# A transformer block in float32 halves: the first 52 feed-forward weight tiles are split ahead of time and kept in DRAM, and the first V step follows 36 U steps instead of 44

## The chip, the cores and the metric

The kernel runs on one core of a Trainium2 chip. The metric is the device time of one execution in microseconds (us). Before the change the median of three runs is 1940.61 us (1940.46 to 1943.16).

A core has four engines that compute here. TensorE (PE in the rows; PEld is its weight load) multiplies matrices, VectorE (DVE) and GpSimd (POOL) work on elements, and ScalarE (ACT) applies functions and copies. SyncE (SP) issues most of the DMAs. Each engine works through its own queue in order and waits on semaphores for the others.

## The reference, cut to what matters

One block of a diffusion transformer: 512 latent tokens and 256 context tokens of 1024 features. A token mixer (an mLSTM in both directions, a window attention, two branch gates) gives the new residual x1. The feed-forward part that the change is about picks experts by product keys, per token and head, and sums their outputs:

```python
def block(xb):                                   # 128 tokens
    q = (xb @ w_query).reshape(128, 8, 2, 128)
    s = jnp.einsum('mhpd,hpnd->mhpn', q, sub_keys)
    s1, i1 = lax.top_k(s[:, :, 0], 16)
    s2, i2 = lax.top_k(s[:, :, 1], 16)
    ...                                          # the 16 best of the 256 sums of pairs
    top, pos = lax.top_k(cand, 16)
    idx = jnp.take_along_axis(cidx, pos, axis=-1)
    g = jax.nn.softmax(top, axis=-1)
    act = jax.nn.gelu(jnp.einsum('mhkd,md->mhk', expert_u[idx], xb))
    return jnp.einsum('mhk,mhkd->md', g * act, expert_v[idx])
```

There are 128 x 128 = 16384 experts, each a row of u and a row of v of 1024 features.

## The kernel before, in words

Every large product is made in float32 precision from two halves. A weight tile of 128 x 1024 is loaded raw (512 KB), its high half is a rounded copy made by ScalarE, its low half is the difference, made by VectorE or GpSimd. Three matmuls (high by high, low by high, high by low; `mm3`, lines 161 to 164) then stand for one. Raw tiles lie in the tag `wraw` with 4 buffers (`WR`), high halves in `whi` with 3 and low halves in `wlo` with 3. The mixer and the feed-forward part share these buffers.

The mixer (lines 96 to 671) has no order written by hand: a planner takes, of the instructions that can run, the one that comes first in the code. A load of weights can run as soon as a raw buffer is free, so loads come early and wait for buffers. The mixer's weight tiles are, in this order, those of the input projection (`project`, `gate_proj`; line 230 and line 581), 8 of the merge (line 624) and 8 of w_out (line 659). Then x1 is normed and split into `h2hi`, `h2lo`.

From line 740 on each engine works in the order of emission. TensorE's order is `stream` (lines 675 to 680): 16 Q steps (query columns of one half head), then `N1 + 2` = 46 U steps (u of 128 experts by 384 tokens, 24 matmuls), then V 44, U 46, V 45, U 47 and so on in pairs (V: v of 128 experts, 18 matmuls), and at last the V steps that have no U beside them: 126, 127 and 0 to 43. The activations of the first `N1` U tiles (`gelu`, line 1025) are stored to DRAM in groups of four and read again for their V.

A step's tile is loaded four steps ahead (`load`, `LA`), and split two steps ahead by `high` (ScalarE, line 701) and `low` (line 707). `low` works on GpSimd for the first 60 steps and on VectorE afterwards.

VectorE's work beside the steps is emitted by generators, along three estimated clocks (`clk`): `background` finds the 16 best of each list (`top16`, lines 771 to 778; 24 calls), `choose` (line 810) turns places into expert numbers and weights for each of the four blocks of 128 tokens, and `weights` (line 865) builds one-hot rows for three blocks, which TensorE multiplies in 48 groups of 16 small matmuls (line 921). The result, a weight for each dense token and each expert, goes through DRAM (`Gd`). `choose` lets GpSimd make one product (line 838) for three of the four blocks. No V step can begin before all weights are there. The fourth block's tokens are not dense: for them the 128 + 128 chosen rows of u and v are gathered one by one (`gather`, `rows`), spread over the V steps at an estimated 3.1 us each, and VectorE works on each row (lines 999 and 1007).

Of the kernel before, what the change touches and what calls it, by code (L numbers as in the profile page):

```python
# [3 lines left out]

# [24 lines left out]
SB = 1  # L29
N1 = 44  # L30
# [3 lines left out]
LA, GB = 4, 6  # L34


def body(ctx, tc, A, out):
# [43 lines left out]
    class Pair:  # L81
        """[128, 8, n] as two tiles of four chunks"""
# [92 lines left out]
    a1 = cst.tile([128, 16], F32, name="a1")     # gain, gain of the context  # L175
# [47 lines left out]
    aqd = dr.tile([128, NB, 512], F32, name="aqd")      # waits for the attention  # L223
    nc.sync.dma_start(aqd, aqt)
# [1 line left out]
    def wtiles(src, col, n, eng=None):  # L226
        """src [1024, ncols] -> four tiles [128, 2, n] raw, split in two."""
# [8 lines left out]
    def project(col, n, feat, tok, eng=None):  # L236
        """feat: list of (feature-tile offset) computed as [feat, T] for the latent tokens;
        tok: list of blocks computed as [tok, n]"""
# [17 lines left out]

    kT = ga([128, NH, T], F32, "kT")
    pf, _ = project(cK, 512, range(4), [], G)
    for h in range(4):
        S.activation(kT[:, h], pf[h], AF.Copy, scale=KSCALE)  # L260
# [9 lines left out]
    # gates, attention k and v (token layout)  # L270
# [15 lines left out]
    # log sigmoid of the forget gates, li and lf zero-padded by direction  # L286
    zz = wk.tile([128, 6, 2, 2, 8], F32, name="zz", bufs=1)  # blk, dir, kind, (dir h)
# [46 lines left out]
    # back to columns; (dir, quantity, head) on the free axis  # L334
# [9 lines left out]
    # natural order: by block, for the backward direction un-reversed  # L344
    ct = cst.tile([128, 6, 2, 4, 4], F32, name="ct")     # blk, dir, quantity, head
# [18 lines left out]
    # mlstm k, v  # L364
# [29 lines left out]
    for h in range(4):  # L394
# [38 lines left out]
        adas(16 + 3 * h, 19 + 3 * h)  # L433
    den = wk.tile([128, 2, 4, 4], F32, name="den", bufs=1)
# [31 lines left out]
    # rotation tables with the gains in: (q, k), (cos, sin), block, 64  # L466
# [8 lines left out]
    # queries and keys as exact halves stacked on the contraction axis:  # L475
    # kv head 0 has [hi; lo], kv head 1 has [lo; hi]
# [45 lines left out]
    for n in range(4):  # L522
        # keys in the order context, previous block, own block, next block
# [6 lines left out]
        mx = wk.tile([128, 4, 8], F32, name="mx", tag="mx")   # max, -max, den, sink term  # L530
# [42 lines left out]
        adas(28 + 5 * n, 33 + 5 * n)  # L573

# [3 lines left out]
    def gate_proj(col, dst):  # L578
        """sigmoid of 128 columns of the input projection, feature layout"""
# [10 lines left out]
    # o gate, then m (feature layout)  # L590
    sigo = gate_tile("sigo")
    for h in range(4):
        gate_proj(cO + h * 128, sigo[:, h])
    g_m = load_const("g_mlstm", [128, 4])
# [9 lines left out]
    # the branch gates wait in DRAM  # L604
    sgd = dr.tile([8, 128, 2, T], F32, name="sgd")
    for n in range(8):
        for br in range(2):
            st = gen.tile([128, T], F32, name="sgs", tag="SGS", bufs=2)
            gate_proj(cG + br * 1024 + n * 128, st)
            nc.sync.dma_start(sgd[n, :, br], st)  # L610

    V.tensor_tensor(out=mod[:, 16:48], in0=mod[:, 16:48], in1=b_ada[:, 16:48], op=ALU.add)

# [4 lines left out]
    for n in range(8):  # L618
# [23 lines left out]
        split(zh[n // 4][:, n % 4], zl[n // 4][:, n % 4], z0)  # L642
    g1 = mod[:, 16:24]
    x1T = Pair(F32, T, "x1T")
    x1d = dr.tile([128, 4, D], F32, name="x1d")     # token layout, for the end
# [40 lines left out]
    raws, his, los = {}, {}, {}  # L686

    def load(j):
        if j >= NS:
            return  # L690
        kind, i = stream[j]
        t = raws[j] = wp.tile([128, 1024], F32, name="wraw", tag="wraw", bufs=WR)
# [5 lines left out]
    def high(j):  # L698
        if j < NS:
# [3 lines left out]
    def low(j):  # L703
        if j < NS:
            los[j] = wp.tile([128, 1024], F32R, name="wlo", tag="wlo", bufs=3)
            pool = j < 16 + N1
            (G if pool else V).tensor_tensor(out=los[j], in0=raws.pop(j), in1=his[j].bitcast(F32), op=ALU.subtract)  # L707
            if pool:
                clk["P"] = max(clk["P"], clk["T"]) + 2.2
            else:  # L710
                clk["D"] = max(clk["D"], clk["T"]) + 1.1

    for j in range(LA):
        load(j)
    for j in range(3):
        high(j)
        low(j)
# [6 lines left out]
    TS = SB * 128                       # tokens whose experts are gathered  # L724
    TD = T - TS                         # tokens that meet every expert
# [41 lines left out]
    def top16(srcs, val, idx):  # L767
        """the 16 largest, in order, of each row of srcs [128, 4, n]"""
# [41 lines left out]
    def choose(b):  # L810
        """the 16 experts of each head for block b -> [128 tokens, (i1, i2, weight), 128 picks]"""
# [19 lines left out]
        # one-hot of the list position, laid out [head, list position, pick]  # L831
        ohs = []
        for c in range(2):
# [3 lines left out]
            eng = V if b == ORDER[0] else G  # L837
            eng.tensor_tensor(out=oh, in0=oh, in1=idv[:, :, c, :, None].to_broadcast([128, 8, 16, 16]), op=ALU.mult)
            if eng is G:
                clk["P"] = max(clk["P"], clk["D"] + 1.2) + 4.3  # L840
            ohs.append((oh, clk["P"] if eng is G else 0.0))
            yield 1.15 if eng is G else 2.3
# [6 lines left out]
        for c, (oh, ready) in enumerate(ohs):  # L849
            yield ("until", ready + 0.3)  # L850
# [11 lines left out]
    peq = deque()                        # (estimated time, PE work)  # L862
    actq = deque()

    def weights(b):
        pick = picks[b]
        w = pa_([128, 4, 128], F16, "pT16", bufs=2)
        we = pa_([128, 128], BF16, "pTe", bufs=2)
        st = {}

        def tr():
# [3 lines left out]
            return 0.4  # L875

        def tr2():
            p = st["p"]
            S.activation(w[:, 0:2], p[:, 0:2], AF.Copy)
            gs = st["gs"] = pa_([128, 128], F32, "gs")  # L880
# [440 lines left out]
```

## Time and profile before

| | before |
|---|---|
| median of three runs | 1940.61 us |
| span of the profiled execution (no other time of it is given) | 1938.4 us |
| mean granted TensorE clock | 0.966 |
| busy: TensorE / VectorE / ScalarE / GpSimd | 1789.8 / 1491.4 / 718.2 / 689.3 us |
| moved by DMA | 427 MB, 220 GB/s in the mean |
| GpSimd, low halves of line 707 | 60 instructions, 193.4 us |

Busy time of an engine is the time in which an instruction of it runs. TensorE's matmuls overlap and their ends are modelled, so the distance from one start to the next tells more than a duration. The clock is a share of 2.4 GHz. The stages of the span: the mixer up to about 594 us, the Q steps to about 690 us, U steps and one-hot products to 1040 us, pairs of V and U to 1722 us, lone V steps to 1926 us, and the last sums and stores.

### The profile page before, as it was taken

How to read it: one execution, taken by the hardware profiler on the slowest of the kernel's cores; microseconds unless marked ns; L12 is line 12 of the kernel's file. 1: busy time of each engine (PE TensorE's matmuls, PEld its weight loads, DVE VectorE, ACT ScalarE, POOL GpSimd, SP SyncE). 2: the span in 40 equal slices, each digit the busy share in tenths (PEclk: the TensorE clock that was granted, in tenths of full speed). 3: DMA queues.
4: the chain of work that ended last, by engine and by line, in shares of the span. 5: the costliest groups of instructions: out<-in, count | busy, mean ns of one | idle time of the engine just before them, and what ended most of it. 6: DMA issues, size and time to landing. Idle time of an engine off the chain costs nothing.

```text
span 1938.4 us, 24739 instructions
## 1 busy us (share of the span) xinstructions
PE 1789.8 (92%) x9039; PEld 1536.8 (79%) x9039; DVE 1491.4 (77%) x2710; ACT 718.2 (37%) x1087; POOL 689.3 (36%) x477
## 2 busy tenths in 40 slices
PE   3798998998989986889899999999999999999997
PEld 2586876555878876889799999999999999987775
DVE  7968688445647999959685777778778788878887
ACT  4242355444334333334343333333333333333332
POOL 2440254120213546546634334333333333333431
PEclk9898998999999997899999999999999999999999
DMA  8276212222533233266579888888888889889884
GB/s 348 84 248 221 86 50 83 59 66 71 169 120 129 77 103 109 93 195 202 179 220 338 319 308 318 300 315 305 315 308 310 316 302 319 302 323 349 340 346 167
DMA packets 197467, 426.97 MB, mean 220 GB/s; under 512 B 13536, under 2 KB 105312, under 8 KB 195936
## 3 DMA queue, kind: packets, MB, share of 16 engines
q1 hardware_dynamic: 109360, 257.32, 37.5%
q0 software_dynamic: 36864, 134.23, 19.3%
q10 hardware_dynamic: 51120, 33.82, 5.7%
q8 instruction: 71, 1.16, 0.2%
q14 instruction: 52, 0.43, 0.1%
HBM read 382.07 MB, written 43.25 MB: 219 GB/s over the span
## 4 chain that ended last, share of the span: by engine, by line
PE 63%; DVE 25%; issue 4%; DMA 3%; ACT 3%; POOL 2%; SPq 0%; ACTq 0%; DVEq 0%; POOLq 0%
PE pu L163 8%; PE pu L164 8%; PE pu L162 8%; PE pa L163 7%; PE pa L164 7%; PE pa L162 7%; PE pg L921 4%; PE ps L162 3%; PE ps L164 3%; PE ps L163 3%; POOL wlo L707 2%; DVE wada L119 2%; PE a L570 2%; DVE ids L774 2%; DVE tokh L1007 2%
## 5 line engine op out<-in xcount | busy, mean ns | idle before, releaser
L163 PE MATMUL pu<-h2hi,wlo 128*128 128x384 f32 (+1 forms) x1152 | 399.8, 347 | 17.0 <-POOL wlo L707 17.0
L162 PE MATMUL pu<-h2hi,whi 128*128 128x384 f32 (+1 forms) x1152 | 405.9, 352 | 6.9 <-ACT St L1032 4.2
L164 PE MATMUL pu<-h2lo,whi 128*128 128x384 f32 (+1 forms) x1152 | 399.8, 347 | 0.0
L707 DVE TENSOR_TENSOR wlo<-wraw,whi 128x1024 fp32r<-128x1024 f32 x212 | 259.5, 1224 | 135.5 <-ACT whi L701 135.0
L163 PE MATMUL pa<-whi,wl 128*128 128x512 f32 x768 | 303.4, 395 | 5.0 <-DVE wl L1048 4.1
L162 PE MATMUL pa<-whi,wh 128*128 128x512 f32 x768 | 300.7, 392 | 5.9 <-ACT wh L1044 5.8
L164 PE MATMUL pa<-wlo,wh 128*128 128x512 f32 x768 | 301.3, 392 | 0.0
L701 ACT ACTIVATE whi<-wraw 128x1024 fp32r<-128x1024 f32 x272 | 285.6, 1050 | 36.3 <-issue 23.7
L707 POOL TENSOR_TENSOR wlo<-wraw,whi 128x1024 fp32r<-128x1024 f32 x60 | 193.4, 3232 | 216.7 <-ACT whi L701 216.5
L975 POOL DMA_INDIRECT gath<-in_v,idx x128 | 155.3, 1213 | 278.5 <-DVE tokh L1007 261.6
L975 POOL DMA_INDIRECT gath<-in_u,idx x128 | 152.1, 1188 | 271.5 <-DVE gw L999 256.3
L163 PEld LDWEIGHTS pu<-h2hi,wlo 128*128 128x128 f32 x1152 | 222.0, 193 | 26.0 <-POOL wlo L707 18.2
L162 PEld LDWEIGHTS pu<-h2hi,whi 128*128 128x128 f32 x1152 | 222.4, 193 | 15.8 <-ACT St L1032 4.5
L164 PEld LDWEIGHTS pu<-h2lo,whi 128*128 128x128 f32 x1152 | 221.1, 192 | 5.5 <-DVE h2lo L50 0.4
L50 POOL TENSOR_TENSOR wlo<-wraw,whi 128x1024 fp32r<-128x1024 f32 (+1 forms) x36 | 88.7, 2465 | 265.2 <-ACT whi L49 256.3
L163 PEld LDWEIGHTS pa<-whi,wl 128*128 128x128 f32 x768 | 144.4, 188 | 40.7 <-DVE wl L1048 12.6
L162 PEld LDWEIGHTS pa<-whi,wh 128*128 128x128 f32 x768 | 144.7, 188 | 38.4 <-ACT wh L1044 10.1
L164 PEld LDWEIGHTS pa<-wlo,wh 128*128 128x128 f32 x768 | 144.6, 188 | 29.6
L1007 DVE SCALAR_TENSOR_TENSOR tokh<-gath,gw,tokh 128x1024 f32<-128x1024 f32 x127 | 162.4, 1279 | 0.0
L999 DVE CUSTOM_DVE_ANT_0 gath<-gath,tokh 128x1024 f32<-128x1024 f32 x128 | 156.1, 1219 | 2.1 <-DMA gath<-in_u,idx 2.1
L1044 ACT ACTIVATE wh<-act 128x384 fp32r<-128x384 f32 x84 | 44.2, 526 | 262.2 <-DVE act L1040 262.2
L162 PE MATMUL ps<-hhi,whi 128*128 128x512 f32 x224 | 98.0, 437 | 21.6 <-ACT hhi L49 21.6
(337 smaller groups left out, 2929.3 us busy)
## 6 DMA issues: line engine op xcount, KB each, us to landing
wraw<-in_uT SPq DMA_DIRECT2D x128, 512.0 KB, 4.9
wraw<-in_v SPq DMA_DIRECT2D x128, 512.0 KB, 6.2
Gd<-stg ACTq DMA_DIRECT2D x24, 1024.0 KB, 7.4
Gt<-Gd SPq DMA_DIRECT2D x32, 768.0 KB, 6.6
wraw<-in_w_in SPq DMA_DIRECT2D x40, 512.0 KB, 4.1
wada<-in_w_adaT SPq DMA_DIRECT2D x32, 512.0 KB, 4.4
Sd<-St ACTq DMA_DIRECT2D x11, 768.0 KB, 5.1
St<-Sd SPq DMA_DIRECT2D x11, 768.0 KB, 5.4
```

The costliest lines, as they stand in the source:

```text
L50: (eng or V).tensor_tensor(out=lo, in0=src, in1=hi.bitcast(F32), op=ALU.subtract)
L119: V.tensor_tensor_reduce(out=junk, in0=w, in1=silp[:, i], scale=1.0, scalar=0.0, op0=ALU.mult, op1=ALU.add, accum_out=col)
L162: PE.matmul(p, sh, mh, start=first, stop=False)
L163: PE.matmul(p, sl, mh, start=False, stop=False)
L164: PE.matmul(p, sh, ml, start=False, stop=last)
L701: S.activation(his[j], raws[j], AF.Copy)
L707: (G if pool else V).tensor_tensor(out=los[j], in0=raws.pop(j), in1=his[j].bitcast(F32), op=ALU.subtract)
L921: PE.matmul(p[:, ti], oa[:, ti // 4, :, ti % 4], ob[c][:, ti // 4, :, ti % 4], start=(c == 0), stop=(c == 1))
L975: G.indirect_dma_start(out=t, out_offset=None, in_=sparse["src"][s // 128], in_offset=bass.IndirectOffsetOnAxis(ap=sparse["idx"][:, s // 1 ...
L999: V.tensor_tensor_reduce(out=t, in0=t, in1=tokh[:, 0], scale=1.0, scalar=0.0, op0=ALU.mult, op1=ALU.add, accum_out=gw[:, 0, s:s + 1])
L1007: V.scalar_tensor_tensor(out=tokh[:, 1], in0=t, scalar=gw[:, 0, s - 128:s - 127], in1=tokh[:, 1], op0=ALU.mult, op1=ALU.add)
L1044: S.activation(wh, acts[i], AF.Copy)
```

## The change

Three things change.

1. `ahead(n)` makes the halves of the next n of the first `JP` = 52 steps' tiles (16 Q, 36 U): load, high half by ScalarE, low half by VectorE into the raw tile itself, and two stores to the DRAM tensor `halves`. It is called at places all through the mixer, and each of its instructions gets a place 2000 later (`LATER`) in the planner's order than where it stands. In the feed-forward part the first 52 steps load both halves from DRAM straight into `whi` and `wlo`, two steps ahead, without `high` and `low`. The later steps are as before, with `low` on VectorE alone.
2. `N1` goes from 44 to 36: 38 U steps come before the first V, 90 pairs follow, then 38 lone V.
3. VectorE makes all products of line 838, the transposes of the picks (`turn`) are emitted right after each choice, and two estimates change: a U step's eighth from 0.49 to 0.515, a group of one-hot matmuls from 1.0 to 1.9.

Comments were taken out too. The diff, cut to its core:

```diff
-N1 = 44
+N1 = 36
+JP, LATER = 16 + N1, 2000
...
+    halves = dr.tile([JP, 128, 2, 1024], F32, name="halves")
+    presplit = iter(range(JP))
+
+    def ahead(n):
+        for j in list(islice(presplit, n)):
+            with tc.high_priority(offset=-LATER):
+                raw = wp.tile([128, 1024], F32, name="sraw", tag="wraw", bufs=WR)
+                src = A["w_q"][j] if j < 16 else A["uT"][j - 16].rearrange("p k n -> p (k n)")
+                nc.sync.dma_start(raw, src)
+                hi = wp.tile([128, 1024], F32R, name="shi", tag="whi", bufs=3)
+                S.activation(hi, raw, AF.Copy)
+                V.tensor_tensor(out=raw.bitcast(F32R), in0=raw, in1=hi.bitcast(F32), op=ALU.subtract)
+                nc.sync.dma_start(halves[j, :, 0], hi.bitcast(F32))
+                nc.sync.dma_start(halves[j, :, 1], raw)
...
     pf, _ = project(cK, 512, range(4), [], G)
+    ahead(2)
...
         V.tensor_tensor(out=gk[:, b], in0=px[b][:, 256:272], in1=bg, op=ALU.add)
+    ahead(4)
...
         adas(16 + 3 * h, 19 + 3 * h)
+        ahead(4)
...
         adas(28 + 5 * n, 33 + 5 * n)
+        ahead(4)
...
         gate_proj(cO + h * 128, sigo[:, h])
+        ahead(1)
...
             nc.sync.dma_start(sgd[n, :, br], st)
+            ahead(1)
...
         split(zh[n // 4][:, n % 4], zl[n // 4][:, n % 4], z0)
+        ahead(1)
...
         kind, i = stream[j]
+        if j < JP:
+            his[j] = wp.tile([128, 1024], F32R, name="whi", tag="whi", bufs=3)
+            los[j] = wp.tile([128, 1024], F32R, name="wlo", tag="wlo", bufs=3)
+            for c, t in enumerate((his[j], los[j])):
+                nc.sync.dma_start(t.bitcast(F32), halves[j, :, c])
+            return
...
     def high(j):
-        if j < NS:
+        if JP <= j < NS:
...
     def low(j):
-        if j < NS:
+        if JP <= j < NS:
             los[j] = wp.tile([128, 1024], F32R, name="wlo", tag="wlo", bufs=3)
-            pool = j < 16 + N1
-            (G if pool else V).tensor_tensor(out=los[j], in0=raws.pop(j), in1=his[j].bitcast(F32), op=ALU.subtract)
...
-    for j in range(LA):
-        load(j)
-    for j in range(3):
-        high(j)
-        low(j)
+            V.tensor_tensor(out=los[j], in0=raws.pop(j), in1=his[j].bitcast(F32), op=ALU.subtract)
+            clk["D"] = max(clk["D"], clk["T"]) + 1.1
+
+    nxt = [0]
+
+    def loads(j):
+
+        while nxt[0] <= j + (2 if nxt[0] < JP else LA):
+            load(nxt[0])
+            nxt[0] += 1
+
+    loads(0)
...
-            eng = V if b == ORDER[0] else G
-            eng.tensor_tensor(out=oh, in0=oh, in1=idv[:, :, c, :, None].to_broadcast([128, 8, 16, 16]), op=ALU.mult)
...
+            V.tensor_tensor(out=oh, in0=oh, in1=idv[:, :, c, :, None].to_broadcast([128, 8, 16, 16]), op=ALU.mult)
+            ohs.append(oh)
+            yield 2.4
...
-                    return 1.0
+                    return 1.9
...
             flags.add(("pick", b))
+            if b >= SB:
+                turn(b)
...
-    cost = {"Q": 0.65, "U": 0.49, "V": 0.65}
+    cost = {"Q": 0.65, "U": 0.515, "V": 0.65}
...
-                load(j + LA)
+                loads(j)
```

## Rows read from the trace of the kernel before

**Rows 1.** Busy time by stretch: PE, PEld, DVE, ACT, POOL (count), clock, DMA share, GB/s

```profile
461.00:566.00 105.00, 99.19 (x434) 76.93 (x435) 56.70 (x62) 33.56 (x46) 13.48 (x10) 0.98 0.45 143
566.00:594.60 28.60, 21.64 (x88) 17.63 (x87) 15.71 (x20) 14.18 (x23) 4.00 (x2) 0.82 0.13 40
594.60:700.00 105.40, 105.39 (x548) 91.63 (x548) 96.63 (x675) 39.28 (x55) 54.04 (x73) 1.00 0.31 109
700.00:866.00 166.00, 129.12 (x760) 124.26 (x759) 146.23 (x274) 57.91 (x87) 89.93 (x35) 0.86 0.38 126
866.00:1040.00 174.00, 164.76 (x1093) 157.73 (x1090) 131.70 (x179) 70.36 (x117) 87.55 (x25) 0.97 0.66 208
1040.00:1721.70 681.70, 681.60 (x3445) 620.23 (x3445) 542.93 (x665) 239.75 (x330) 243.77 (x208) 1.00 0.88 316
1721.70:1926.00 204.30, 193.51 (x812) 151.53 (x811) 171.42 (x187) 66.00 (x90) 59.15 (x45) 0.99 0.81 309
1840.00:1880.00 40.00, 39.26 (x172) 31.61 (x171) 36.24 (x41) 13.92 (x19) 15.68 (x12) 1.00 0.96 376
```

**Rows 2.** ScalarE in order of time, query steps: start, us, line, output<-input [idle <-releaser]

```profile
594.61 1.28 ACT L787 ACTIVATE qs<-pu 128x512 f32<-128x512 f32 x2 [3.64 <-PE pu L164]
...
615.60 0.60 ACT L787 ACTIVATE qs<-pu 128x512 f32<-128x512 f32 x1 [0.79 <-PE pu L164]
...
660.02 0.60 ACT L787 ACTIVATE qs<-pu 128x512 f32<-128x512 f32 x1 [0.76 <-PE pu L164]
```

**Rows 3.** TensorE in order of time: U matmuls, the first V, the last pair's end

```profile
1027.68 0.33 PE L163 MATMUL pu<-h2hi,wlo 128*128 128x384 f32 x1
...
1039.82 0.34 PE L164 MATMUL pu<-h2lo,whi 128*128 128x384 f32 x1
1040.13 0.49 PE L162 MATMUL pa<-whi,wh 128*128 128x512 f32 x1
...
1721.74 0.39 PE L162 MATMUL pa<-whi,wh 128*128 128x512 f32 x1
...
1725.64 0.39 PE L164 MATMUL pa<-wlo,wh 128*128 128x512 f32 x1
```

**Rows 4.** Chain of waits, 690 to 1045 us: start, us, engine, what

```profile
713.26 0.29 DVE pf L817
...
716.18 4.37 DVE pos1h L838
...
721.72 2.29 DVE pos1h L838
...
728.11 1.92 DVE pick L857
...
756.60 3.59 DVE em L891
...
770.77 0.60 DVE oa L907
...
840.64 1.90 PE pg L921 x16
...
948.13 13.53 POOL wlo L707
```

**Rows 5.** Waits from 585 to 1040 us: who waited for whom, us, times, longest

```profile
PE pg L921 <- DVE ob L914: 18.4, 7, 9.0
...
PE pu L163 <- POOL wlo L707: 17.0, 4, 7.6
```

**Rows 6.** DMA issues of the weights' store: count, KB each, us to landing

```profile
Gd<-stg ACTq DMA_DIRECT2D x24, 1024.0 KB, 7.4
```

**Rows 7.** Instruction groups, whole span: count, busy us, mean ns, idle before

```profile
L701 ACT ACTIVATE whi<-wraw 128x1024 fp32r<-128x1024 f32 x272 | 285.6, 1050 | 36.3 <-issue 23.7 <-DMA wraw<-in_w_q 5.0 <-ACT St L1032 2.8
L707 DVE TENSOR_TENSOR wlo<-wraw,whi 128x1024 fp32r<-128x1024 f32 x212 | 259.5, 1224 | 135.5 <-ACT whi L701 135.0
```

**Rows 8.** Waits of SyncE's DMA queue, 110 to 640 us: us, times, longest

```profile
SPq L659 <- DVE wlo L50: 31.7, 8, 4.2
```

More of the change, by code (lines that the diff above doesn't have):

```diff
@@ L3 @@
 from contextlib import ExitStack
+from itertools import islice
 import numpy as np
@@ L703, in low @@
     def low(j):
-        if j < NS:
+        if JP <= j < NS:
             los[j] = wp.tile([128, 1024], F32R, name="wlo", tag="wlo", bufs=3)
-            pool = j < 16 + N1
-            (G if pool else V).tensor_tensor(out=los[j], in0=raws.pop(j), in1=his[j].bitcast(F32), op=ALU.subtract)
[L708 to L711, printed above, removed]
-    for j in range(LA):
-        load(j)
-    for j in range(3):
-        high(j)
-        low(j)
+            V.tensor_tensor(out=los[j], in0=raws.pop(j), in1=his[j].bitcast(F32), op=ALU.subtract)
[6 more added lines that the diff above has]
+    loads(0)
     a2 = scale_gain("a2", mod[:, 32:40], g_ffn)
@@ L836, in choose @@
                             in1=abf[:, c, :, None, :].to_broadcast([128, 8, 16, 16]), op=ALU.is_equal)
-            eng = V if b == ORDER[0] else G
-            eng.tensor_tensor(out=oh, in0=oh, in1=idv[:, :, c, :, None].to_broadcast([128, 8, 16, 16]), op=ALU.mult)
[L839 to L842, printed above, removed]
+            V.tensor_tensor(out=oh, in0=oh, in1=idv[:, :, c, :, None].to_broadcast([128, 8, 16, 16]), op=ALU.mult)
+            ohs.append(oh)
+            yield 2.4
         tb = top[:, b]
@@ L848, in choose @@
         yield 0.2
-        for c, (oh, ready) in enumerate(ohs):
-            yield ("until", ready + 0.3)
+        for c, oh in enumerate(ohs):
             for n in (8, 4, 2):
@@ L863, in body, with turn @@
     actq = deque()
-    def weights(b):
+    turned = {}
+    def turn(b):
         pick = picks[b]
-        w = pa_([128, 4, 128], F16, "pT16", bufs=2)
-        we = pa_([128, 128], BF16, "pTe", bufs=2)
-        st = {}
+        w = pa_([128, 4, 128], F16, "pT16", bufs=3)
+        st = turned[b] = {"w": w}
         def tr():
@@ L874, in tr @@
                 PE.transpose(p[:, c], pick[:, c], ident)
-            return 0.4
+            return 0.6
         def tr2():
@@ L879, in tr2, with weights @@
             S.activation(w[:, 0:2], p[:, 0:2], AF.Copy)
-            gs = st["gs"] = pa_([128, 128], F32, "gs")
+            gs = pa_([128, 128], F32, "gs", bufs=3)
             S.activation(gs, p[:, 2], AF.Copy, scale=WSCALE)
+            st["gs"], st["when"] = gs, clk["T"] + 1.2
         peq.append((clk["D"] + 0.3, tr, tr2))
+    def weights(b):
+        st = turned[b]
         while "gs" not in st:
             yield None
-        yield ("until", clk["T"] + 1.2)
+        w = st["w"]
+        we = pa_([128, 128], BF16, "pTe", bufs=2)
+        yield ("until", st["when"])
         gu, em = st["gs"].bitcast(U32), pa_([128, 2, 128], U32, "em")
@@ L1165, in body @@
     for j in range(2):
-        load(j + LA)
+        loads(j + 1)
         query_out(j, pq[j])
-    high(3)
-    low(3)
     ps_prev = pq[1]
@@ L1200, in body @@
             if sub == 0:
-                load(j + LA)
+                loads(j)
                 if j > 2 and stream[j - 1][0] == "Q":
```

## The prediction

> **What bounds the kernel now.** I read the table by stage first. From 1040.0 to 1721.7 us TensorE is busy for 681.6 of 681.7 us at granted clock 1.00: nothing there can be gained except by giving TensorE less work, and the change gives it the same matmuls [rows 1]. Time can be gained in three places. From 700 to 866 us TensorE is busy for 129.1 of 166.0 us and its clock averages 0.86, while VectorE is busy for 146.2; from 866 to 1040 us it is busy for 164.8 of 174.0; from 1721.7 to 1926 us for 193.5 of 204.3 [rows 1].
>
> I cut the run at four marks: A = 594.6 us, where the first two query steps have ended [rows 2]; the first V at 1040.1 and the last pair's end at 1721.7 [rows 3]; the last step at about 1926, with a tail of 12.4 us to the span's end at 1938.4. The page gives no other time of the profiled execution; the runs' median lies 2.2 us above the span.
>
> **The stage from A to the first V, before.** A query step takes (660.02 - 615.60) / 7 = 6.35 us [rows 2]. U matmuls start 0.173 us apart ((1039.82 - 1027.68) / 70), so 24 of them make 4.16 us [rows 3]. A group of 16 one-hot matmuls takes 1.90 us; there are 48 [rows 4]. TensorE's floor is 14 x 6.35 + 46 x 4.16 + 48 x 1.90 + some 7 us of small transposes = 378 us. It took 445.5, so 67 are lost. To what: the waits show TensorE waiting for GpSimd's low halves (17.0 us) and for VectorE's one-hot tiles (18.4) [rows 5]; the chain of waits has two stretches of 13.5 and 13.7 us on GpSimd's subtraction, one of them shown [rows 4]. VectorE itself is stretched: L891 on 128x128 elements takes 3.59 us while GpSimd subtracts, against 0.60 for a 128x1024 half-precision product that runs free, and one L838 takes 4.37 where the next takes 2.29 [rows 4].
>
> **Part 1: GpSimd loses the subtractions (57 in this stage) and six L838 products.** VectorE takes the products: 6 x 2.29 = +13.7 us. What it gets back I work out as its floor. The lists of the top 16 end where the choice begins, at 713.0 us, A + 118: VectorE is full up to there and its work on the lists is unchanged [rows 1, 4]. The first choice runs from 713.0 to 730.0 us, 17.1,; without the stretch of one L838 (4.37 - 2.29) and of its last product (1.92 against some 0.3) it is 13.3, so four take 53. The one-hot work is 3 x (some 1.3 + 16 x 5 x 0.605) = 149. After the last group a store of 7.4 us [rows 6], a load of about as much and the first weighting follow, say 20. Floor: 118 + 53 + 149 + 20 = A + 340.
>
> **Part 2: 38 U tiles before the first V, not 46.** Eight U of 4.16 us leave this stage: TensorE's floor falls by 33 to A + 345. They are paired with V later, so there are 90 pairs for 82 and 38 lone V for 46. A pair takes (1721.74 - 1040.13) / 82 = 8.31 us [rows 3], so the pairs take 748 us. A lone V takes 204.3 / 46 = 4.44 us while its 18 matmuls need 4.1 (17 steps of 0.229 us from 1721.74 to 1725.64, and one more) [rows 1, 3]: the gathered rows on VectorE hold it back. 46 x (4.44 - 4.1) = 16 us is all that can be had there. In the chip's time the gather starts some 60 us earlier against a longer pair stage, so I let half of the lone V run free: 19 x 4.44 + 19 x 4.15 = 163 us. Two fewer groups are stored and read again; the DMA share is 0.88 there and no wait hangs on them, so I cost them at nothing (a 1.5 MB store and load at 316 GB/s, 10 us, if they did count).
>
> **Part 3: the 52 early halves ("fillers").** Each loads 0.5 MB, takes 1.05 us of ScalarE and 1.22 us of VectorE [rows 7], and stores 1 MB: 55 and 64 us of engine time and 82 MB, and the loads of the first 52 steps double, 27 MB more. Where they land matters more than their sum. They wait for one of four raw buffers and one of three buffers of high halves, which the mixer's own weights use, and SyncE's loads already wait for those buffers (31.7 us for w_out alone) [rows 8]. The planner gives a filler the place of an instruction 2000 later in the code. Counted in the code, fillers 0 to 9 come among the branch gates and the merge, 10 to 21 among the eight w_out tiles, and 22 to 51 only from about the fourth query step to the fifth U. So I don't take "beside the mixer" at its word: less than half have a place there.
>
> In the mixer: from 461 to 566 us the DMA moves 143 GB/s, 15 MB in 105 us [rows 1]. Sixteen fillers add 25 MB; 40 MB at 376 GB/s, the highest rate of a stretch in my table, is 107 us. So this stretch fills but hardly overflows; with buffers held for each other I take +10 us. Bounds: -5 (the third query step waited for its weights, which now come as halves) and +50 (22 fillers x 2.27 us with nothing hidden). SyncE's queue is in order: a store that waits for VectorE holds back the load behind it, which is why I don't take 0.
>
> In the query stage: VectorE is full there [rows 1], so fillers add to it at full price. I let 24 of the 30 fall there (the others fit in the idle 28 us before A): 24 x 1.22 = 29 us, VectorE's floor A + 369. On TensorE I add 8 us for halves that come late for want of a buffer. Result: first V at A + 377, 32 above TensorE's floor of 345. Bounds: A + 345 and A + 415 (below).
>
> **Sum.** A = 594.6 + 10 = 604.6; first V 981.6; pairs to 1729.7; lone V to 1892.7; tail 12.4: 1905 of span, and 2.2 more: **1907 us**, 1.7% below 1940.6. By terms: 67 - 32 = 35 from the weighting stage, less 10 in the mixer, plus some 8 from the lone V and rounding of the pairs.
>
> **Rivals.** (a) *The fillers hide.* ScalarE and GpSimd are lightly used and from 566 to 594.6 us the DMA moves only 40 GB/s [rows 1]. A unmoved, first V at A + 348, pairs 748, lone V 160, tail 12.4 and 2.2: 1866 us. Against it: places and buffers as above.
>
> (b) *The fillers pile up on the first query steps: slower.* At steps 4 to 20 a filler takes a high-half buffer ahead of the step's own halves. The stretch then moves 17 x 1.05 MB of halves and 26 x 1.57 MB of fillers = 59 MB. At 376 GB/s that is 156 us, where TensorE needs 12 x 6.35 + 5 x 4.16 = 97: 59 us lost. With 15 us in the mixer and 10 of mismatch later, the first V is at 609.6 + 345 + 69 = 1024, and the end at 1024 + 748 + 163 + 12.4 + 2.2 = 1950. It decides once the loss in the query stage passes some 60 us. For it: the buffers are few and TensorE's clock fell to 0.86 in the last stage that starved it. Against it: the halves are not needed so early, and the stretch moved only 109 GB/s before [rows 1]. The Trainium skill, SBUF — State Buffer, section SBUF: two separate sides, speaks against the change here: it names HBM, at about 358 GB/s for one core, as the usual end-to-end limit. By that rate the 59 MB would take 165 us and this rival 9 us more. Two stretches of this trace with 376 and 316 GB/s lie around it, so the trace doesn't settle it.
>
> (c) *The order is off.* Each engine keeps its order of emission, set by estimated times. The estimate for a group of one-hot matmuls becomes 1.9, which is the measured 1.90; but the lists take VectorE 110 us, where the estimate has 24 x 4 = 96, so TensorE meets the first transposes some 14 us before VectorE has them, and the fillers' 29 us aren't in the estimate. If none of that is made up and TensorE falls to its lower clock on the way, 60 of the 67 us stay lost: A + 405, and 1935 to 1940: no change.
>
> **Chances.** The forecast 0.46, (a) 0.27, (b) 0.18, (c) 0.09. No change means within 0.2% (1936.7 to 1944.5), about what a measurement can tell here. Faster: all of the forecast and (a) and a third of (c): 0.76; same 0.06; slower 0.18. The range reaches from (a), 1866, to just past (b), 1954, leaving out the far half of each; the forecast's own range is 1885 to 1930.
>
> **What would show it.** Right: no GpSimd subtraction from L707; VectorE's L891 near 0.3 us; first V between 965 and 1000 us; 38 lone V, the last ones at 4.1 us; A between 595 and 615; about 24 fillers on VectorE after A. Wrong towards (a): nearly all fillers before A. Wrong towards (b): query steps of 9 us and more, waiting for halves from DRAM at a lowered clock. The prediction falls as a whole if the pairs take more than 8.31 us, or if TensorE was not waiting for GpSimd and VectorE in the old stage at all, but for something that the change leaves.

## The result, and the profile after

The changed kernel takes **2044.8 us** (median of 4 runs, 2035.5 to 2048.8) against 1940.5 for the kernel before, beside it on the same chip: a ratio of **1.053 [1.050, 1.056]**. The forecast was 1907 us. The profiled execution has a span of 2040.1 us at a granted clock of 0.942 of full speed; before it was 1938.4.

The table by stretch, cut at the same marks as [rows 1] (columns as there); the first two rows are two stretches of it at the same times, the others follow the marks of the kernel after.

```profile
461.00:566.00 105.00, 92.19 (x387) 65.38 (x386) 37.78 (x61) 44.34 (x65) 26.17 (x11) 0.96 0.71 233
566.00:594.60 28.60, 25.59 (x95) 20.23 (x94) 0.00 (x0) 6.63 (x8) 11.83 (x5) 0.85 0.76 232
...
725.60:840.00 114.40, 114.39 (x600) 100.63 (x600) 108.26 (x759) 24.16 (x39) 15.51 (x64) 1.00 0.57 193
840.00:900.00 60.00, 45.48 (x236) 43.20 (x236) 58.04 (x124) 16.41 (x26) 0.00 (x0) 0.83 0.58 193
900.00:1050.00 150.00, 149.57 (x1104) 140.79 (x1103) 142.49 (x243) 55.58 (x106) 0.00 (x0) 1.00 0.86 261
1050.00:1115.30 65.30, 51.58 (x273) 49.23 (x270) 15.18 (x24) 13.01 (x23) 15.31 (x13) 0.92 0.95 341
1115.30:1866.00 750.70, 750.15 (x3783) 682.46 (x3784) 602.15 (x716) 262.93 (x363) 265.26 (x233) 1.00 0.89 315
1866.00:2027.00 161.00, 155.15 (x661) 126.80 (x661) 113.76 (x129) 55.90 (x74) 16.05 (x12) 0.97 0.65 237
2027.00:2040.10 13.10, 4.99 (x23) 3.79 (x21) 7.50 (x9) 0.00 (x0) 3.82 (x3) 0.83 0.33 121
```

The same four marks, from the views by tile (line, engine, output<-input, count: shortest/median/longest ns, start of the first to start of the last): the gates' sigmoids, attention, w_out, the query steps, the first V, and the fillers' three instructions.

```profile
L612 ACT ACTIVATE sigo<-ps x4: 594/597/597, 455.9 to 492.4; 128x512 f32<-128x512 f32 x4
L612 ACT ACTIVATE sgs<-ps x16: 578/598/599, 504.3 to 611.0; 128x512 f32<-128x512 f32 x16
L590 ACT ACTIVATE pTs<-a x18: 597/597/600, 362.5 to 495.9; 128x512 f32<-128x512 f32 x18
L164 PE MATMUL ps<-zhi,whi x64: 388/392/487, 656.2 to 702.5; 128*128 128x512 f32 x64
...
L164 PE MATMUL pa<-whi,wh x768: 387/389/796, 1115.3 to 2031.1; 128*128 128x512 f32 x192
...
L271 ACT ACTIVATE shi<-sraw x52: 1038/1050/1062, 114.8 to 562.7; 128x1024 fp32r<-128x1024 f32 x52
L273 SPq DMA_DIRECT2D halves<-shi x52: 319/326/1033, 115.9 to 566.5; - x52
L272 DVE TENSOR_TENSOR sraw<-sraw,shi x52: 1207/1220/2197, 115.9 to 563.8; 128x1024 fp32r<-128x1024 f32 x52
```

A gate "ends" here where its sigmoid starts. Read together: A, where the first two query steps have ended, moved from 594.6 [rows 2] to 725.6 us, **131 later**. From A to the first V it takes 389.7 us for 445.5, 55.8 less. From the first V to the end it takes 924.8 for 898.3, 26.5 more. 131.0 - 55.8 + 26.5 = 101.7, the difference of the spans. So 29.3 us came outside the mixer, where the forecast has some 43, and the mixer lost 131. All 52 fillers ran there, the last at 562.7 us; none after A.

What the mixer lost is seen from two sides. The gates, 20 projections that TensorE does between the pieces of mLSTM and attention, ended at 611.0 us; in a kernel without fillers (e9 below) they end at 457.6 and the o gates begin at 233.4 instead of 455.9. And TensorE stands idle meanwhile. First the kernel after, then e9, the same stretches of 50 us:

```profile
250.00:300.00 50.00, 38.82 (x248) 32.27 (x246) 43.99 (x124) 25.26 (x62) 9.85 (x14) 0.91 0.84 297
300.00:350.00 50.00, 11.97 (x38) 7.58 (x38) 48.29 (x68) 14.61 (x22) 18.75 (x10) 0.50 0.39 142
```

```profile
250.00:300.00 50.00, 41.37 (x215) 33.58 (x213) 44.11 (x77) 22.38 (x41) 35.86 (x26) 0.93 0.23 63
300.00:350.00 50.00, 44.38 (x202) 30.97 (x203) 33.62 (x67) 26.03 (x43) 15.65 (x9) 0.97 0.31 90
```

From 300 to 350 us TensorE is busy for 12.0 of 50 us, with its clock down to 0.50, the lower of its two levels (1.2 GHz), where e9 has 44.4 at 0.97. VectorE, the third busy time of a line, is at 48.3 of 50, and from 250 to 300 us the DMA engines move 297 GB/s, where e9 moves 63. Bytes alone don't empty the stretch from 300 to 350: in e10 below, where 50 of the 52 fillers move none, TensorE is at 21.4 there.

SyncE's queue in order of time (start, us, queue, line, what) shows where the first gate's weights (L605) stand. In the kernel before its loads began at 161 us; after, the first is at 427.55, with stores of fillers (L273, L274) ahead of it.

```profile
421.81 0.32 SPq L273 DMA_DIRECT2D halves<-shi  x1
422.23 2.45 SPq L274 DMA_DIRECT2D halves<-sraw  x3
427.55 0.38 SPq L605 DMA_DIRECT2D wraw<-in_w_in  x1
428.77 0.33 SPq L269 DMA_DIRECT2D sraw<-in_uT  x1
430.01 0.38 SPq L605 DMA_DIRECT2D wraw<-in_w_in  x1
```

And the chain of waits (start, us, what) shows what a gate then waits for: a filler's store, which holds one of the three buffers of high halves that the gate's own copy needs.

```profile
495.40 7.36 DMA halves<-shi
...
502.86 1.07 ACT whi L51
...
504.08 2.39 POOL wlo L52
...
506.93 6.71 DMA halves<-shi
```

### The profile page after: what moved, and what is told of

It reads as the page before. It is cut to its first block, busy times and chain, and to the rows that moved or that the text cites. A ratio compares the mean times of both kernels' runs of the same rounds, so it can differ in the third digit from the quotient of the medians.

```text
span 2040.1 us, 25111 instructions
## 1 busy us (share of the span) xinstructions
PE 1821.1 (89%) x9039; PEld 1553.9 (76%) x9039; DVE 1487.5 (73%) x2776; ACT 703.3 (34%) x1073; POOL 462.2 (23%) x411
## 4 chain that ended last, share of the span: by engine, by line
PE 68%; DVE 18%; DMA 7%; issue 2%; ACT 2%; POOL 1%; ACTq 0%; SPq 0%; DVEq 0%; POOLq 0%
PE pa L165 9%; PE pa L166 9%; PE pa L164 8%; PE pu L164 8%; PE pu L165 8%; PE pu L166 8%; PE pg L958 4%; PE ps L165 3%; PE ps L164 3%; PE ps L166 3%; DVE wada L121 2%; DMA wada<-in_w_adaT 2%; PE a L593 2%; DVE ids L807 1%; DMA halves<-shi 1%
## 5 line engine op out<-in xcount | busy, mean ns | idle before, releaser
L739 DVE TENSOR_TENSOR wlo<-wraw,whi 128x1024 fp32r<-128x1024 f32 x220 | 269.3, 1224 | 169.0 <-ACT whi L734 169.0
L1012 POOL DMA_INDIRECT gath<-in_u,idx x128 | 146.6, 1145 | 509.1 <-DVE gw L1036 261.4
L734 ACT ACTIVATE whi<-wraw 128x1024 fp32r<-128x1024 f32 x220 | 231.0, 1050 | 22.4 <-PE pa L165 11.6
L1012 POOL DMA_INDIRECT gath<-in_v,idx x128 | 148.4, 1159 | 267.6 <-DVE tokh L1044 250.4
L1036 DVE CUSTOM_DVE_ANT_0 gath<-gath,tokh 128x1024 f32<-128x1024 f32 x128 | 156.1, 1221 | 12.4 <-DMA gath<-in_u,idx 12.4
L1081 ACT ACTIVATE wh<-act 128x384 fp32r<-128x384 f32 x92 | 48.4, 526 | 299.9 <-DVE act L1077 290.2
L52 POOL TENSOR_TENSOR wlo<-wraw,whi 128x1024 fp32r<-128x1024 f32 (+1 forms) x36 | 86.8, 2414 | 281.8 <-ACT whi L51 158.8
L1069 ACT ACTIVATE act<-pu 128x384 f32<-128x384 f32 x92 | 45.2, 492 | 195.7 <-PE pu L166 193.5
```

The costliest lines, as they stand in the source:

```text
L52: (eng or V).tensor_tensor(out=lo, in0=src, in1=hi.bitcast(F32), op=ALU.subtract)
L734: S.activation(his[j], raws[j], AF.Copy)
L739: V.tensor_tensor(out=los[j], in0=raws.pop(j), in1=his[j].bitcast(F32), op=ALU.subtract)
L1012: G.indirect_dma_start(out=t, out_offset=None, in_=sparse["src"][s // 128], in_offset=bass.IndirectOffsetOnAxis(ap=sparse["idx"][:, s // 1 ...
L1036: V.tensor_tensor_reduce(out=t, in0=t, in1=tokh[:, 0], scale=1.0, scalar=0.0, op0=ALU.mult, op1=ALU.add, accum_out=gw[:, 0, s:s + 1])
L1069: S.activation(acts[i], p, AF.Gelu_apprx_tanh)
```

## The experiments

All marks in one table, in us of each profiled execution: A, the last branch gate, the first V, the end of the span, and the run's time (the median where it was timed; else one run).

| run | A | last gate | first V | span | time |
|---|---|---|---|---|---|
| before | 594.6 | 458.8 | 1040.1 | 1938.4 | 1940.5 |
| after | 725.6 | 611.0 | 1115.3 | 2040.1 | 2044.8 |
| e1 before + fillers | 728.0 | 610.5 | 1172.5 | 2070.8 | 2072.6 |
| e2 after, 2 fillers | 602.6 | 469.5 | 992.7 | 1915.8 | 1917.6 |
| e3 gates first | 715.8 | 602.3 | 1104.7 | 2026.6 | 2031.9 |
| e4 no offset | 698.3 | 584.4 | 1089.4 | 2009.6 | 2011.4 |
| e5 no stores | 647.2 | 532.3 | 1037.3 | 1959.2 | 1961.4 |
| e6 DMA only | 684.9 | 570.6 | 1075.0 | 1996.9 | 1998.7 |
| e7 engines only | 643.5 | 529.1 | 1034.5 | 1954.9 | 1956.6 |
| e8 rest alone | 597.0 | 462.8 | 1012.3 | 1932.9 | 1936.2 |
| e9 rest, split | 591.9 | 457.6 | 980.7 | 1899.5 | **1905.3** |
| e10 engines, gates first | 639.8 | 527.0 | 1030.7 | 1951.0 | 1952.8 |
| e11 DMA, gates first | 675.1 | 562.1 | 1063.6 | 1985.5 | 1987.3 |
| e12 20 fillers | 611.8 | 478.4 | 999.4 | 1919.8 | 1921.5 |
| e13 small stores | 661.1 | 546.9 | 1052.3 | 1972.6 | 1974.3 |
| e14 ACT's queue | 733.4 | 618.8 | 1123.1 | 2045.0 | 2047.2 |

**e1, the kernel before with the fillers added.**

```diff
--- before
+JP, LATER = 52, 2000
+    ahead(2)
...
+        ahead(4)
...
+            ahead(1)
```

> The kernel before with the 52 early halves made in the mixer exactly as in the change, but the feed-forward part as before: it doesn't read them, and N1 stays 44. All three theories of the mixer's cost (buffers handed out in code order, so that the gates' weights stand behind the early halves; the DMA's 82 MB; the engines' 119 us) say that the two first query steps end near 725 us instead of 594.6, and the time is 1940 + 131 = 2070 us. If the loss belonged to the feed-forward part instead, it would stay near 1940.

2072.6 us: the loss is whole without any other part of the change. A is at 728.0, and from A to the first V it takes 444.5 us as before (445.5).

**e2, the change with 2 of 52 fillers.**

```diff
-        for j in list(islice(presplit, n)):
+        for j in [j for j in islice(presplit, n) if j < 2]:
...
-                nc.sync.dma_start(t.bitcast(F32), halves[j, :, c])
+                nc.sync.dma_start(t.bitcast(F32), halves[j % 2, :, c])
```

> The changed kernel with only the first two tiles' halves made early; the first 52 steps all load these two tiles' halves again and again, so the output is not the reference's, while the feed-forward part has the same instructions and the same loads. The mixer should end as before (594.6 us) and the rest should keep its gain: 2040 - 131 = 1909 us, with 1911 as a run's time. If the gain of the feed-forward part came only because the mixer had been stretched, it would be 1940 or more.

1917.6 us, 23 below the kernel before; A to the first V takes 390.1 us, as with the change (389.7). A itself is at 602.6, 8 us after the kernel before, with two fillers left. The feed-forward part keeps its gain; e1 and e2 together put the loss on the fillers and on the mixer.

**e3, the gates ahead of the fillers in code** (three calls behind each gate, none earlier), **and e4, no offset.**

```diff
-    ahead(2)
...
-        ahead(4)
...
         gate_proj(cO + h * 128, sigo[:, h])
-        ahead(1)
+        ahead(3)
```

```diff
-JP, LATER = 16 + N1, 2000
+JP, LATER = 16 + N1, 0
```

> The changed kernel, with all calls of ahead moved behind the gate projections in the code, three tiles after each of the 20 gates instead of 38 tiles ahead of them; the same 52 tiles are made, with the same 2000 places later. Theory of the buffers' order: the gates' weights get their buffers as in the kernel before, their matmuls fill TensorE beside mLSTM and attention again, and the first two query steps end between 600 and 640 us: 1915 to 1955 us. Theories of DMA traffic or of engine time: the same 82 MB and 119 us fall into a shorter stretch, so it ends no earlier than 715: 2030 us or more.

> The changed kernel with LATER = 0: the early halves keep their places in the code. Theory of the buffers' order: the gates still stand behind 38 of them, but these are done sooner, so part of the loss goes: first query steps end between 670 and 715 us, 1985 to 2030 us. Theory of engine time: they now go ahead of mLSTM and attention instructions, so it gets worse, above 2050. Theory of DMA traffic: no change, 2040.

e3 took 2031.9 us (ratio to before 1.048 [1.046, 1.050]): the theory that the gates are late because 38 fillers stand ahead of them fell. The o gates were on time again (232.5 to 269.6), and the branch gates still ended at 602.3. e3's chain of waits, by columns as above, shows why: the same wait for a store now stands between each gate and the next, some 20 us apart.

```profile
504.89 4.95 DMA halves<-shi
509.95 1.06 ACT whi L51
511.14 2.35 POOL wlo L52
...
522.29 1.48 ACT shi L271 x2
523.77 7.04 DMA halves<-shi
530.91 1.06 ACT whi L51
532.10 2.35 POOL wlo L52
```

e4 gave 33 us back and lies in the range of the order theory (1985 to 2030), which e3 contradicts; so order may have a part, but it isn't the whole. The offset of 2000 changes which instruction an engine takes first; it did not move any filler out of the mixer in either kernel.

**e5, e6, e7: a filler taken apart.** e5 leaves out the stores, e6 the engines' work, e7 loads and stores. As in e2, the steps of e5 and e7 (and of e10 and e13) read the halves of the first two tiles over and over.

```diff
--- e5
+                if j < 2:
-                nc.sync.dma_start(halves[j, :, 0], hi.bitcast(F32))
+                    nc.sync.dma_start(halves[j, :, 0], hi.bitcast(F32))
...
--- e6
-                hi = wp.tile([128, 1024], F32R, name="shi", tag="whi", bufs=3)
-                S.activation(hi, raw, AF.Copy)
-                V.tensor_tensor(out=raw.bitcast(F32R), in0=raw, in1=hi.bitcast(F32), op=ALU.subtract)
-                nc.sync.dma_start(halves[j, :, 0], hi.bitcast(F32))
+                nc.sync.dma_start(halves[j, :, 0], raw)
...
--- e7
-                nc.sync.dma_start(raw, src)
+                if j < 2:
+                    nc.sync.dma_start(raw, src)
+                    src = raw
+                else:
+                    src = silp[:, 0]
...
```

> The changed kernel with its 52 early tiles still loaded and split beside the mixer, but only the first two written to DRAM; the feed-forward steps all read those two (so the steps use wrong weights). Left out: 50 pairs of stores, 50 x 1.05 MB. Theory H (a filler holds its high-half buffer until its store has landed, and the gates' tiles wait in the same rotation of 3; with the stores gone it is held some 2.3 us, one ACT copy and one VectorE subtraction, instead of 8 to 10): the mixer comes back most of the way, 1930 to 1965 us, the branch gates end by 520 us of the span. Theory D (the bytes beside the mixer cost the time; 27 of 82 MB are left): a third of the 131 us stays, about 1960. Theory E (the 52 ACT copies and 52 VectorE subtractions in those engines' queues, 55 and 64 us): nothing comes back, 2030 or more.

> The changed kernel with the early tiles' loads and both stores (the raw tile is written twice), but without the ACT copy, the subtraction and the high-half buffer (both halves in DRAM are the raw tile, so the feed-forward part computes with wrong weights). All 82 MB stay, in the order of the queue. Theory H: the high-half rotation is free, and only the four raw buffers are still shared, each held through one load and two stores: 1935 to 1985 us. Theory D: 2035 to 2050, as with the change. Theory E: 1915 to 1930, since no ACT or VectorE work is left.

> The changed kernel with 50 of its 52 early tiles made from a tile that lies in SBUF all the time: the ACT copies, subtractions and both buffers stay, the loads and stores go (the feed-forward steps read the halves of the first two, so they use wrong weights). Theory H: a high-half buffer is held only through a copy and a subtraction, so 1925 to 1960 us. Theory D: 1915 to 1925. Theory E: 2020 or more.

1961.4, 1998.7 and 1956.6 us. None of the three theories holds alone: H's range holds in e5 and e7 and D's in e5, but e6 lies outside all three. Against e2, the engines' work costs 39 us (e7), and loads and stores without any engine work cost 81 (e6); 39 + 81 = 120 of the 127 us that the 50 fillers cost together. The loads add 5 (e5 over e7), which single runs can't tell from nothing: the four runs of the change lie 13 us apart. Holding the high-half buffers (theory H) is not needed for the 81 us: e6 uses none. Its fillers still hold a raw buffer each, through one load and two stores.

**e10, e11: the same two halves with the gates first.** The edits of e7 and e6 with that of e3.

> As e7 (50 of the early tiles made from a tile that lies in SBUF, no loads and stores for them; the feed-forward steps use the wrong halves), but with the calls moved behind the gates' projections, three per gate, as in e3. e7 took 1957, 39 us above e2. Theory O (these 39 us are order: 38 fillers stand ahead of the first gate in the rotation of the buffers, first o gate at 360 instead of 234): they go, 1918 to 1932. Theory E (they are the time of the ACT copies and VectorE subtractions): they stay, 1948 or more.

> As e6 (loads and both stores of the raw tile, no ACT copy, subtraction or high-half buffer; wrong halves), but with the calls moved behind the gates' projections, three per gate. e6 took 1999, 81 us above e2. Theory O: order alone, so 1918 to 1945. Theory B (bytes: three fillers of 1.57 MB stand between two gates, 4.7 MB or some 15 to 18 us at the 260 to 330 GB/s that the traces show, where the gates of the kernel before went at one per 11.7 us): the last branch gate is near 282 + 15 x 16 to 20 = 520 to 580, and the run takes 1965 to 2025.

e10 took 1952.8, 4 us below e7 and no clear difference: the 39 us of engine work do not go with the fillers' places in the code. Its stretch by stretch table has the place:

```profile
250.00:300.00 50.00, 41.57 (x224) 33.40 (x222) 42.70 (x90) 36.46 (x59) 23.90 (x21) 0.90 0.25 74
300.00:350.00 50.00, 21.41 (x96) 16.02 (x95) 41.96 (x70) 21.34 (x33) 17.30 (x9) 0.66 0.10 27
```

TensorE is busy for 63.0 of these 100 us, where e9, without fillers, has 85.8 and e2, with two, 83.2. VectorE's busy time doesn't tell them apart: 84.7 in e10, 77.7 in e9, but 84.7 in e2 too. Attention's first transposed tile comes at 361.0 for 333.2 in e9 and 344.0 in e2. The waits of TensorE from 200 to 560 us (who waited for whom: us, times, longest) have the name of it, first in e10, then in e2:

```profile
PE a L530 <- DVE akv L526: 17.4, 3, 9.3
PE a L587 <- DVE sm L581: 13.8, 4, 6.4
```

```profile
PE a L528 <- DVE akv L524: 7.5, 3, 4.5
PE a L585 <- DVE sm L579: 7.4, 5, 2.2
```

What TensorE lacks meanwhile is gates. e10's rows of ScalarE and VectorE in order of time (start, us) have a gate's high half (L51), those of three fillers (L275), the first of the fillers' subtractions (L276) and the next gate's high half:

```profile
292.42 1.05 ACT L51 ACTIVATE whi<-wraw 128x1024 fp32r<-128x1024 f32 x1
294.44 1.99 ACT L275 ACTIVATE shi<-sil 128x1024 fp32r<-128x1024 f32 x2
307.86 1.05 ACT L275 ACTIVATE shi<-sil 128x1024 fp32r<-128x1024 f32 x1
329.53 1.22 DVE L276 TENSOR_TENSOR sraw<-sil,shi 128x1024 fp32r<-128x1024 f32 x1
...
336.80 1.06 ACT L51 ACTIVATE whi<-wraw 128x1024 fp32r<-128x1024 f32 x1
```

The three subtractions start at 329.53, 332.23 and 334.45, behind mLSTM's and attention's work on VectorE. Until its own is done a filler holds a high-half buffer; there are three, they pass on in the order of the code, and no gate is split for 44 us, where e9 and e2 split four each. In the change itself no filler is subtracted from 301.71 to 339.08 us. So theory H seems to have a part in the 39 us; no run here measures it.

e11 took 1987.3, inside what theory B gave, 11 below e6. Its branch gates are (562.1 - 282.2) / 15 = 18.7 us apart, in e9 (457.6 - 281.8) / 15 = 11.7. The three fillers between two gates are 3 x 1.57 = 4.7 MB, 18 us at the 252 to 263 GB/s of the rows below. That is the distance between the gates: the fillers' transfers pace them. In e11's chain of waits the load of a gate takes 5.2 to 6.9 us (four of them, from 480 to 540 us), where the median of the kernel before is 3.7 from issue to landing. Waits of gate loads for a raw buffer that a store holds add up to 5.0 us there. TensorE is idle meanwhile (e11, columns as above):

```profile
450.00:500.00 50.00, 30.33 (x111) 20.09 (x109) 7.30 (x11) 9.10 (x13) 4.69 (x2) 0.80 0.71 252
500.00:550.00 50.00, 19.59 (x52) 14.01 (x53) 0.00 (x0) 6.45 (x7) 8.11 (x4) 0.66 0.78 263
```

**e13, e14: bytes or queue.**

```diff
--- e13
+                m = 1024 if j < 2 else 128
-                nc.sync.dma_start(halves[j, :, 0], hi.bitcast(F32))
+                nc.sync.dma_start(halves[j, :, 0, 0:m], hi[:, 0:m].bitcast(F32))
...
--- e14
-                nc.sync.dma_start(halves[j, :, 0], hi.bitcast(F32))
+                nc.scalar.dma_start(halves[j, :, 0], hi.bitcast(F32))
```

> The changed kernel, but of 50 of the 52 early tiles only the first 128 of 1024 columns of each half are stored: the same number of stores, in the same order and with the same waits, at an eighth of the bytes (the feed-forward steps read the halves of the first two, so they use wrong weights). Theory B (the bytes of the stores cost the 81 us): the time falls to that of e5, which had no stores, 1955 to 1975 us. Theory Q (it is SyncE's queue, where a store waits for ACT or VectorE and the loads behind it wait too): it stays at 2015 to 2050.

> The changed kernel with both stores of an early tile issued from ACT's queue instead of SyncE's; all bytes stay. Theory Q: loads no longer stand behind waiting stores, so 1960 to 2000 us, unless ACT, which now waits for VectorE's subtraction before the second store, gives it back. Theory B: 2030 to 2060, as with the change.

1974.3 and 2047.2 us: theory B on both counts. With the same 104 stores at an eighth of their bytes 70 of the 83 us between e5 and the change are gone; the other 13, between single runs, may go with the stores' number, waits and remaining 6.6 MB. With all bytes, another queue changes nothing on balance; e14 alone would leave room for a gain that ScalarE gives back, since the second store now waits there for VectorE, but e13, which keeps SyncE's queue, does not. The Trainium skill says the same (DMA: Bandwidth & Descriptors, section Issuing engines are not separate DMA queues): whichever engine starts a DMA, it runs on the same 16 DMA engines, and only the sequencer's time to start it is saved. 2047.2 against 2044.8 agrees.

**e8, e9, e12: what the early halves were worth.** e8 is the change without them: the first 52 tiles raw, copied on ACT, subtracted on GpSimd. e9 gives GpSimd only the first 28 of them and VectorE the other 24. e12 is e9 with 20 tiles made early, one filler behind each gate.

```diff
--- e8, against the kernel before
-N1 = 44
+N1 = 36
...
-            eng = V if b == ORDER[0] else G
-            eng.tensor_tensor(out=oh, in0=oh, in1=idv[:, :, c, :, None].to_broadcast([128, 8, 16, 16]), op=ALU.mult)
+            V.tensor_tensor(out=oh, in0=oh, in1=idv[:, :, c, :, None].to_broadcast([128, 8, 16, 16]), op=ALU.mult)
...
+            if b >= SB:
+                turn(b)
--- e9, against e8
-            pool = j < 16 + N1
+            pool = j < 16 + 12
```

> The change without the early halves: 36 U steps ahead of the first V, the one-hot products on VectorE, each block turned as soon as it is chosen, the new estimates of the U step; but the first 52 weight tiles are loaded raw, copied on ACT and subtracted on GpSimd as before. The mixer is then that of the kernel before (first query steps ended near 595 us). If the early halves are not needed for the earlier first V (GpSimd keeps up, since its six one-hot products are gone), the first V is near 595 + 390 = 985 and the end 925 later: 1908 to 1925 us, faster than both. If GpSimd's subtractions at 2.3 us and more hold the query and U steps up again, the first V is at 595 + 430 or more: 1945 or more. Between them: some of both.

> As e8 (the rest of the change without early halves), but GpSimd makes the low halves of only the first 28 weight tiles; those of the other 24 U tiles go to VectorE, 24 x 1.22 = 29 us more there. In e8 single subtractions of GpSimd took up to 24 us while VectorE made the one-hot rows, and TensorE waited 18 us for them; first V at 1012. Theory P (GpSimd is slowed by VectorE's work beside it, and that held the U steps up): the first V is bounded by VectorE, near 595 + 340 + 29 = 964 to 985, the end 1890 to 1912. Theory V (VectorE has no room: what GpSimd loses is added there): first V at 1010 or later, 1930 or more.

> e9 with the first 20 of its tiles made early: 20 fillers, all of them behind the first gate in code, one after each gate. Theory of order and bytes: one filler (1.57 MB, some 5 us of the DMA engines) fits between two gates that are 11.7 us apart, so the mixer loses 0 to 15 us, the branch gates end by 475, and the run is within -5 to +15 us of e9. If each filler costs a share of the whole (127 us over 52): 49 us above e9.

e8: 1936.2 us, ratio to before 0.997 [0.996, 0.998]; A to the first V 415.3. The cause, which e9 tests, is in GpSimd's row of time: 33.75 us for three subtractions beside VectorE's one-hot rows. Two of the three took 2.4 us and one 29.1 (the expectation of e9 has up to 24); it ended in the first pause of VectorE's rows, the 6.04 us before 948.98. In e9, where GpSimd subtracts ahead of them, the mean is 2395 ns (columns: start, us, line; then durations in ns, shortest/median/longest; then a group's count, busy us and mean):

```profile
916.07 33.75 POOL L713 TENSOR_TENSOR wlo<-wraw,whi 128x1024 fp32r<-128x1024 f32 x3 [7.99 <-ACT whi L707]
...
948.98 1.38 DVE L931 TENSOR_TENSOR ob<-oc,pT 128x1024 f16<-128x1024 f16 x1 [6.04 <-PE pg L938]
```

```profile
L713 POOL TENSOR_TENSOR wlo<-wraw,whi x3: 2371/2372/29079, 916.1 to 947.4; 128x1024 fp32r<-128x1024 f32 x3
```

```profile
L713 POOL TENSOR_TENSOR wlo<-wraw,whi 128x1024 fp32r<-128x1024 f32 x25 | 59.7, 2395 | 82.6 <-ACT whi L707 82.6
```

That GpSimd is shut out agrees with the Trainium skill (SBUF — State Buffer, section Who interferes with whom): a VectorE instruction with two SBUF inputs contends with a GpSimd instruction that reads SBUF, and one of them waits whole.

e9: **1905.3 us, ratio to before 0.983 [0.982, 0.985]**, the fastest kernel here, and it leaves nothing out. A to the first V takes 388.8 us, as with the change (389.7), and the mixer is untouched. So the early halves bought nothing that 24 subtractions on VectorE don't buy. e12: 1921.5, 16.2 above e9's median and 12 to 20 above its four runs: about the 15 that was given, and far from 49. A is 19.9 later, and the branch gates end at 478.4, not by 475. Fewer fillers cost less than their share of the whole, but these 20 gained nothing either.

## Why the prediction was wrong

**The step that failed is the mixer's term of part 3: "with buffers held for each other I take +10 us. Bounds: -5 ... and +50".** It measured +131. The other terms, as sums, stand nearly as they were, one of them by luck (below): 1905 of span, + 121 in the mixer, + 12.7 to the first V, + 1.2 from there to the end is 2039.9; the span is 2040.1.

- *Place.* I had the planner's 2000 as a place in the code and let 30 of 52 fillers fall behind A ("22 to 51 only from about the fourth query step"). All ran from 114.8 to 562.7 us: the offset did not keep them out. "I don't take 'beside the mixer' at its word" was the wrong way round.
- *The stretch.* I sized the term on 461 to 566 us alone [rows 1], with 16 fillers of 25 MB. There it hardly overflows, as I said. The loss lies at 200 to 560 us, where TensorE is busy for 271.4 of 360 us and in e9 for 331.6; the gates' weights have to come there, with the fillers' 82 MB ahead of them or between them. e5, e13 and the change give the price of the stores: 647.2, 661.1 and 725.6 us for A.
- *Whose slack.* My upper bound, +50, was "22 fillers x 2.27 us with nothing hidden": engine time, for 22 of 52. But TensorE's slack is the thing spent. The gates are its work for the gaps of a chain that runs over VectorE; when their weights are late, the gaps stay empty and the gates come after the chain: attention's last transposed tile moved by 27.6 us (468.3 in e9, 495.9), the last gate by 153.
- *VectorE.* I counted 1.22 us per filler in the query stage, where VectorE is full, and at nothing in the mixer. From 250 to 350 us it has 84.7 of 100 us of work in e2 already; a filler waits there with its buffer held, and the engines' part alone costs 39 us (e7, e10).

**What held.** GpSimd has no subtraction from L707's successor, and VectorE's L891 [rows 4, 3.59 us] takes 0.22. That last sign says little: two of its three rows took 0.23 us before, too. VectorE's lists, choices and one-hot rows ended near 1050, A + 325, where the forecast's floor has A + 320 for them and 20 more to the first V. The pairs take 750.7 / 90 = 8.34 us (8.31); by its own sign the prediction falls above 8.31, but this is 2.7 us in all and not what failed. The 38 lone V take 161.0 (163), the tail 13.1 (12.4).

**What came near by luck.** The first V at A + 389.7 is 12.7 past the A + 377 of the forecast, but those 377 had 24 fillers in them. None was left there, and for that case the forecast's terms give A + 348, rival (a): this stage is 42 us off. TensorE was idle for 14.5 us from 840 to 900 and 13.7 from 1050 to 1115, with the clock at 0.83 and 0.92. The 20 us from the last one-hot row to the first V became 65. In this second stretch the halves of two tiles a step, the first V's weights and the gathered rows together fill the DMA engines (0.95, 341 GB/s); TensorE waited 5.5 us for low halves there by name, and two loads of them stand in the chain of waits (start, us, what):

```profile
1072.35 11.18 DMA wlo<-halves
...
1089.63 11.17 DMA wlo<-halves
```

e9, which loads half as much for these steps, gets there no sooner, so these loads aren't the bound by themselves, and the cause of the 42 us stays open.

**The rivals.** Slower came, but not by (b): the query steps are 6.35 us long and never waited for halves. (b) had the right resource, bytes of fillers against bytes that are needed, in the wrong stage and for the wrong weights. (a) needed a mixer with free engines; each was free on the mean, but not where the gates or attention needed it. Its sign, nearly all fillers before A, came true, and the kernel was slower for it: the sign told the place and not the price. (c) showed in part, from 840 to 900 us: TensorE waited 13.5 us for VectorE's picks ahead of the transposes, close to the 14 that (c) names, and its clock fell (who waited for whom: us, times, longest):

```profile
PE pg L905 <- DVE pick L882: 13.5, 5, 7.1
```

**Open.** The bytes' 70 to 81 us (e13, e6) are not divided further between waiting for a buffer that a slow store holds and waiting behind bytes on the DMA engines; e3's chain shows the first, e11's slower gate loads the second. Nor is the engines' 39 us divided between the work on VectorE and ScalarE and the buffers that the fillers hold while they wait for it. Most of these parts are differences of single runs. Fillers with buffers of their own, and fillers placed behind the mixer's last weights, were not tried.

## What to carry to other kernels

A stage in which every engine looks half idle can still have no room: ask which queue of work fills the gaps of its chain (here the gates on TensorE), and what its operands wait for. Work moved to an earlier stage costs the bytes and buffers that this work needs there, so price it from the loads and the buffers that it displaces, not from its engines' mean, and mind that work of low priority can hold its buffers longer; and before sending halves through DRAM, look for an engine that can make them in place in the stage itself, which here took one condition (e9 against e8) and moved the ratio to the kernel before from 0.997 to 0.983.

## Not expected of the hardware

- Low priority for the fillers did not protect the rest: with the offset of 2000 the kernel takes 2044.8 us, with none 2011.4.
- GpSimd's subtraction of 128x1024 has a mean of 2.4 us in e9; in e8, where VectorE makes one-hot rows, one took 29.1 us and its two neighbours 2.4. A busy GpSimd says little about the work that it does.
- Of the 83 us that the 104 stores cost, 70 go with 7/8 of the bytes of 50 tiles (45.9 MB): 1.5 us for each MB, half of the 2.9 us that a MB takes at 341 GB/s, the highest rate of a stretch in the first table. By this estimate the other half was hidden beside the mixer's work.
